# A row-mean kernel rewritten with its own semaphores, behind an empty tile context, with one engine waiting at the end

## The chip, the cores and the metric

The kernel runs on one core of a Trainium2 chip. The metric is the device time of one execution in microseconds (us). Each comparison alternates a kernel with the kernel before on the same chip; medians of the fast runs are quoted. The "span" is the time from the first to the last recorded instruction of an execution; "time outside the span" is the device time less the span.

## The reference

```python
x = np.random.randn(32, 512, 1024).astype(np.float32)      # 67.1 MB
def reference(x):
    return np.mean(np.maximum(x, 0), axis=-1).astype(np.float32)   # 32 x 512
```

16,384 rows of 1024 numbers are clipped at zero and averaged. The output is 64 KB.

## The kernel before

Each of the 128 partitions holds 128 rows. Seven loads of 8.4 MB (16 rows for each partition) go through three buffers; the eighth is cut into pieces of 8, 4, 2 and 1 rows, and the last row into three column pieces. ScalarE takes the even rows, VectorE the odd ones; each does clip and sum in one instruction. GpSimd multiplies the sums by 1/1024, except for the last row, whose final step VectorE does.

```python
    for t in range(full):
        xt = in_pool.tile([P, NB, D], F32, name="xt")
        nc.sync.dma_start(out=xt, in_=xr[:, j0:j0 + NB, :])
        rows(xt, 0, NB, j0)
    # ... row pieces, then column pieces of 512, 256, 256 into `last` ...
    act_row(nc, last[:, :512], last[:, D:D + 1])
    dve_row(nc, last[:, 512:768], last[:, D + 1:D + 2])
    nc.vector.scalar_tensor_tensor(
        out=last[:, 768:], in0=last[:, 768:], scalar=0.0, in1=scale, op0=ALU.max, op1=ALU.mult,
        accum_out=res[:, J - 1:J])       # reads both partial sums, which stand behind the row
    nc.sync.dma_start(out=outr, in_=res)
    pools.close()
    tc.close()          # the close of the tile context ...
    tc.compile()        # ... whose instructions the trace puts at this line, 134
    issue_ahead_of_entry_barrier(nc)     # moves the first load ahead of the entry barrier
```

All semaphores (counters by which one engine waits for another, or for a transfer) are put in by the tile framework. Its close makes SyncE wait for every outstanding semaphore, lets all engines meet, has GpSimd clear the semaphores, and lets all engines meet again.

## Time and profile before

| | before |
|---|---|
| time, median (range) | 163.88 us (163.78 to 164.01) |
| span of the profiled run, its time | 161.80 us, 163.58 us |
| outside the span | 1.78 us |
| DMA engines busy | 96.9% of the span |
| VectorE, ScalarE busy | 74.3 us, 69.2 us |
| second column piece landed, store issued, store landed, span ends | 158.20, 159.36, 160.90, 161.80 us |

The loads fill the span; the ends of it are what a change of semaphores can reach. The prediction shows the lines.

### The profile page before, as it was taken

What the parts mean: (1) busy time and instruction counts of PE and PEld (TensorE: products, weight loads), DVE (VectorE), ACT (ScalarE), POOL (GpSimd) and SP (SyncE); (2) the same over time, 40 slices, a digit from 0 to 9 for tenths busy, and PEclk for the clock granted to TensorE, in tenths of its full rate; (3) what the DMA queues carried; (4) which work ended last, traced back from release to release, by engine and by line L of the source; (5) the groups of instructions that cost most, each with busy time, mean ns of one, the idle gap of its engine ahead of it and who ended that gap; (6) DMA issues with size and microseconds to landing.
All of it is one profiled execution on the core that took longest, in us unless ns stands there. A gap on an engine that the chain in (4) does not pass through costs nothing.

```text
span 161.8 us, 351 instructions
## 1 busy us (share of the span) xinstructions
DVE 74.3 (46%) x132; ACT 69.2 (43%) x131; POOL 1.3 (1%) x8
## 2 busy tenths in 40 slices
DVE  0000049800696008940099202990049800698992
ACT  3000049600694008920099002980049600696882
POOL 1000000000000000000000000000000000000000
DMA  7997997997998998998998998997997996998990
GB/s 259 518 470 308 518 470 308 518 470 324 502 470 356 470 470 356 470 470 356 470 470 360 470 470 356 470 486 340 470 486 340 470 502 300 462 429 381 421 353 20
DMA packets 2162, 67.19 MB, mean 415 GB/s; under 512 B 240, under 2 KB 624, under 8 KB 880
## 3 DMA queue, kind: packets, MB, share of 16 engines
q1 hardware_dynamic: 2160, 67.18, 96.9%
q14 instruction: 2, 0.02, 0.0%
HBM read 67.11 MB, written 0.07 MB: 415 GB/s over the span
## 4 chain that ended last, share of the span: by engine, by line
DMA 84%; DVE 12%; SPq 1%; issue 0%; DVEq 0%
DMA xt<-in_x_dram 56%; DMA last<-in_x_dram 29%; DVE xt L20 11%; SPq L105 1%; SPq L109 0%; DVE last L20 0%; DVE last L126 0%; DVEq L126 0%; DVEq L20 0%; SPq L97 0%; DVEq L134 0%
## 5 line engine op out<-in xcount | busy, mean ns | idle before, releaser
L20 DVE TENSOR_SCALAR_CACHE_REDUCE xt<-xt 128x1024 f32<-128x1024 f32 x64 | 73.4, 1208 | 84.5 <-DMA xt<-in_x_dram 84.2
L15 ACT ACTIVATE xt<-xt 128x1024 f32<-128x1024 f32 x64 | 66.2, 1036 | 88.6 <-DMA xt<-in_x_dram 88.4
L15 ACT ACTIVATION_READ_ACCUMULATOR xt<-xt 128x1 f32 x64 | 12.0, 187 | 0.0
L20 DVE DVE_READ_ACCUMULATOR xt<-xt 128x1 f32 x64 | 5.3, 82 | 0.0
L90 POOL TENSOR_SCALAR res<-sums 128x112 f32<-128x112 f32 (+1 forms) x2 | 0.5, 251 | 155.9 <-DVE xt L20 155.9
L15 ACT ACT_TABLE_LOAD x1 | 1.3, 1283 | 0.8 <-PEq L150 0.8
L15 ACT ACTIVATE last<-last 128x512 f32<-128x512 f32 x1 | 0.6, 629 | 0.0
L20 DVE TENSOR_SCALAR_CACHE_REDUCE last<-last 128x256 f32<-128x256 f32 x1 | 0.4, 420 | 0.2 <-DMA last<-in_x_dram 0.2
L126 DVE SCALAR_TENSOR_TENSOR last<-last,scale 128x258 f32<-128x258 f32 x1 | 0.4, 430 | 0.2 <-DVE last L20 0.2
L81 POOL MEMSET scale<- 128x258 f32 x1 | 0.3, 314 | 0.3 <-POOLq L150 0.3
L121 POOL TENSOR_SCALAR res<-part 128x1 f32<-128x1 f32 x1 | 0.3, 267 | 0.6 <-DVE xt L20 0.6
L15 ACT ACTIVATION_READ_ACCUMULATOR last<-last 128x1 f32 x1 | 0.2, 186 | 0.0
L150 POOL MEMSET const-bfloat16-1.0<- 128x1 bf16 x1 | 0.1, 103 | 0.0
L150 POOL MEMSET const-uint8-127<- 128x1 uint8 x1 | 0.1, 103 | 0.0
L150 POOL MEMSET const-float32-0.0<- 128x1 f32 x1 | 0.1, 99 | 0.2 <-issue 0.2
L150 POOL MEMSET const-float32-1.0<- 128x1 f32 x1 | 0.1, 99 | 0.0
L126 DVE DVE_READ_ACCUMULATOR last<-last,scale 128x1 f32 x1 | 0.1, 86 | 0.0
L20 DVE DVE_READ_ACCUMULATOR last<-last 128x1 f32 x1 | 0.1, 83 | 0.0
## 6 DMA issues: line engine op xcount, KB each, us to landing
xt<-in_x_dram SPq DMA_DIRECT2D x1, 4096.0 KB, 39.0
xt<-in_x_dram SPq DMA_DIRECT2D x1, 2048.0 KB, 43.5
xt<-in_x_dram SPq DMA_DIRECT2D x1, 1024.0 KB, 45.5
xt<-in_x_dram SPq DMA_DIRECT2D x1, 512.0 KB, 46.4
last<-in_x_dram SPq DMA_DIRECT2D x1, 256.0 KB, 46.5
last<-in_x_dram SPq DMA_DIRECT2D x2, 128.0 KB, 42.7
xt<-in_x_dram SPq DMA_DIRECT2D x7, 48.8
out_dram<-res SPq DMA_DIRECT2D x1, 64.0 KB, 1.5
```

The source lines that it names most:

```text
L15: nc.scalar.activation(out=src, in_=src, func=ACT.Relu, accum_out=acc)
L20: nc.vector.tensor_scalar(out=src, in0=src, scalar1=0.0, scalar2=init, op0=ALU.max, op1=ALU.add, accum_out=acc,)
L81: nc.gpsimd.memset(scale, inv)
L90: nc.gpsimd.tensor_scalar(out=res[:, lo:hi], in0=sums[:, lo:hi], scalar1=inv, scalar2=0.0, op0=ALU.mult, op1=ALU.add,)
L105: nc.sync.dma_start(out=xt[:, lo:lo + n, :], in_=xr[:, j0 + lo:j0 + lo + n, :])
L121: nc.gpsimd.tensor_scalar(out=res[:, J - 2:J - 1], in0=part[:, 0:1], scalar1=part[:, 1:2], scalar2=inv, op0=ALU.add, op1=ALU.mult,)
L126: nc.vector.scalar_tensor_tensor(out=last[:, 768:], in0=last[:, 768:], scalar=0.0, in1=scale, op0=ALU.max, op1=ALU.mult, accum_out=res[:, ...
L150: nc = _bacc.Bacc("TRN2", target_bir_lowering=False, num_devices=1)
```

## The change

The intent is to shed the framework's close. The tile context is closed and compiled while it is still empty; after it the same loads and instructions are written with hand-placed semaphores, one for each load, and at the end SyncE alone waits for the store. The core of the diff:

```diff
+    tc.close()
+    tc.compile()
 ...
+    loaded = [nc.alloc_semaphore(f"loaded{i}") for i in range(full + len(row_pieces) + len(col_pieces))]
+    act, dve, pool = (nc.alloc_semaphore(n) for n in ("act", "dve", "pool"))
+    stored = nc.alloc_semaphore("stored")
+    def load(i, dst, src):
+        nc.sync.dma_start(out=dst, in_=src).then_inc(loaded[i], 16)
+    def buf_free(t):
+        if t >= BUFS:
+            nc.sync.wait_ge(act, t - BUFS + 1)
+            nc.sync.wait_ge(dve, t - BUFS + 1)
 ...  (rows and finish wait on `loaded`, `act` and `dve`; all loads are written first)
+    nc.vector.wait_ge(loaded[i + 2], 16)
+    dve_row(nc, last[:, 512:768], last[:, D + 1:D + 2]).then_inc(dve, 1)
+    nc.vector.wait_ge(act, n_done + 1)
+    nc.vector.wait_ge(dve, n_done + 1)
+    nc.vector.wait_ge(loaded[i + 3], 16)
     nc.vector.scalar_tensor_tensor(
 ...
-    nc.sync.dma_start(out=outr, in_=res)
-    pools.close()
-    tc.close()
-    tc.compile()
+    nc.sync.wait_ge(pool, 2)
+    nc.sync.wait_ge(dve, n_done + 2)
+    nc.sync.dma_start(out=outr, in_=res[:, :]).then_inc(stored, 16)
+    used = [s.num for s in (*loaded, act, dve, pool)]
 ...
+    nc.sync.sem_clear(range(used[0], used[-1] + 1))
+    nc.sync.wait_ge(stored, 16).then_inc(stored, -16)
```

More of the change, by code (lines that the diff above doesn't have):

```diff
@@ L13, in act_row @@
 def act_row(nc, src, acc):
-    nc.scalar.activation(out=src, in_=src, func=ACT.Relu, accum_out=acc)
+    return nc.scalar.activation(out=src, in_=src, func=ACT.Relu, accum_out=acc)
 def dve_row(nc, src, acc, init=None):
-    nc.vector.tensor_scalar(
+    return nc.vector.tensor_scalar(
         out=src, in0=src, scalar1=0.0, scalar2=init,
@@ L38, in issue_ahead_of_entry_barrier @@
     assert first.engine == mybir.EngineType.SP and not first.sync_info.on_wait
-    assert all(i.opcode == "DMACopy" or i.engine != first.engine for i in body[:load])
+    assert all(i.opcode in ("Drain", "EventSemaphore") or i.engine != first.engine for i in body[:load])
     del body[load]
@@ L60 @@
     outr = out.flatten().rearrange("(p j) -> p j", p=P, j=J)
-    xlast = xr[:, J - 1, :]
     NB = 16
+    BUFS = 3
     full = J // NB - 1
@@ L69, with sbuf, rows, finish @@
     assert sum(col_pieces) == D
-    pools = ctx.enter_context(ExitStack())
-    in_pool = pools.enter_context(tc.tile_pool(name="in", bufs=3))
-    res_pool = pools.enter_context(tc.tile_pool(name="res", bufs=1))
-    sums = res_pool.tile([P, J], F32)
-    res = res_pool.tile([P, J], F32)
-    part = res_pool.tile([P, 2], F32)
-    last = res_pool.tile([P, D + 2], F32)
-    scale = res_pool.tile([P, D // 4 + 2], F32)
-    nc.gpsimd.memset(scale, inv)
-    def rows(xt, lo, n, j0):
+    def sbuf(name, *shape):
+        return ctx.enter_context(nc.sbuf_tensor(name, list(shape), F32))
+    bufs = [sbuf(f"rows{b}", P, NB, D) for b in range(BUFS)]
+    sums, res, part = sbuf("sums", P, J), sbuf("res", P, J), sbuf("part", P, 2)
+    last = sbuf("last", P, D + 2)
+    scale = sbuf("scale", P, D // 4 + 2)
+    loaded = [nc.alloc_semaphore(f"loaded{i}") for i in range(full + len(row_pieces) + len(col_pieces))]
[7 more added lines that the diff above has]
+            nc.sync.wait_ge(dve, t - BUFS + 1)
+    for t in range(full):
+        buf_free(t)
+        load(t, bufs[t % BUFS][:, :, :], xr[:, t * NB:(t + 1) * NB, :])
+    j0 = full * NB
+    buf_free(full)
+    xt = bufs[full % BUFS]
+    lo, i = 0, full
+    for n in row_pieces:
+        load(i, xt[:, lo:lo + n, :], xr[:, j0 + lo:j0 + lo + n, :])
+        lo, i = lo + n, i + 1
+    c = 0
+    for w in col_pieces:
+        load(i, last[:, c:c + w], xr[:, J - 1, c:c + w])
+        c, i = c + w, i + 1
+    nc.gpsimd.memset(scale[:, :], inv).then_inc(pool, 1)
+    def rows(i, xt, lo, n, j0):
+        nc.scalar.wait_ge(loaded[i], 16)
+        nc.vector.wait_ge(loaded[i], 16)
         for k in range(lo, lo + n):
             j = j0 + k
-            (dve_row if j % 2 else act_row)(nc, xt[:, k, :], sums[:, j:j + 1])
-    def finish(lo, hi):
+            done = (dve_row if j % 2 else act_row)(nc, xt[:, k, :], sums[:, j:j + 1])
+            if k >= lo + n - 2:
+                done.then_inc(dve if j % 2 else act, 1)
+    def finish(after, lo, hi):
+        nc.gpsimd.wait_ge(act, after)
+        nc.gpsimd.wait_ge(dve, after)
         nc.gpsimd.tensor_scalar(
@@ L92, in finish @@
         )
+    nc.vector.wait_ge(pool, 1)
     for t in range(full):
-        j0 = t * NB
-        xt = in_pool.tile([P, NB, D], F32, name="xt")
-        nc.sync.dma_start(out=xt, in_=xr[:, j0:j0 + NB, :])
-        rows(xt, 0, NB, j0)
-    j0 = full * NB
-    xt = in_pool.tile([P, NB, D], F32, name="xt")
-    prev = xt[:, NB - 2, :]
-    lo = 0
-    for n in row_pieces:
-        nc.sync.dma_start(out=xt[:, lo:lo + n, :], in_=xr[:, j0 + lo:j0 + lo + n, :])
-        lo += n
-    c = 0
-    for w in col_pieces:
-        nc.sync.dma_start(out=last[:, c:c + w], in_=xlast[:, c:c + w])
-        c += w
@@ L112 @@
-    finish(0, j0)
-    lo = 0
-    for n in row_pieces[:-1]:
-        rows(xt, lo, n, j0)
-        lo += n
-    finish(j0, j0 + lo)
-    act_row(nc, prev[:, :448], part[:, 0:1])
-    dve_row(nc, prev[:, 448:], part[:, 1:2])
+        rows(t, bufs[t % BUFS], 0, NB, t * NB)
+    finish(full, 0, j0)
+    lo, i = 0, full
+    for n in row_pieces[:-1]:
+        rows(i, xt, lo, n, j0)
+        lo, i = lo + n, i + 1
+    finish(i, j0, j0 + lo)
+    prev = xt[:, NB - 2, :]
+    nc.scalar.wait_ge(loaded[i], 16)
@@ L121 @@
+    act_row(nc, prev[:, :448], part[:, 0:1]).then_inc(act, 1)
+    nc.vector.wait_ge(loaded[i], 16)
+    dve_row(nc, prev[:, 448:], part[:, 1:2]).then_inc(dve, 1)
+    n_done = i + 1
+    nc.gpsimd.wait_ge(act, n_done)
+    nc.gpsimd.wait_ge(dve, n_done)
     nc.gpsimd.tensor_scalar(
         out=res[:, J - 2:J - 1], in0=part[:, 0:1], scalar1=part[:, 1:2], scalar2=inv, op0=ALU.add, op1=ALU.mult,
-    )
-    act_row(nc, last[:, :512], last[:, D:D + 1])
-    dve_row(nc, last[:, 512:768], last[:, D + 1:D + 2])
+    ).then_inc(pool, 1)
@@ L126 @@
+    nc.scalar.wait_ge(loaded[i + 1], 16)
+    act_row(nc, last[:, :512], last[:, D:D + 1]).then_inc(act, 1)
+    nc.vector.wait_ge(loaded[i + 2], 16)
[3 more added lines that the diff above has]
+    nc.vector.wait_ge(loaded[i + 3], 16)
     nc.vector.scalar_tensor_tensor(
-        out=last[:, 768:], in0=last[:, 768:], scalar=0.0, in1=scale, op0=ALU.max, op1=ALU.mult,
+        out=last[:, 768:], in0=last[:, 768:], scalar=0.0, in1=scale[:, :], op0=ALU.max, op1=ALU.mult,
@@ L128 @@
         accum_out=res[:, J - 1:J],
-    )
-    nc.sync.dma_start(out=outr, in_=res)
-    pools.close()
-    tc.close()
-    tc.compile()
+    ).then_inc(dve, 1)
+    nc.sync.wait_ge(pool, 2)
+    nc.sync.wait_ge(dve, n_done + 2)
+    nc.sync.dma_start(out=outr, in_=res[:, :]).then_inc(stored, 16)
+    used = [s.num for s in (*loaded, act, dve, pool)]
+    assert used == list(range(used[0], used[0] + len(used)))
+    nc.sync.sem_clear(range(used[0], used[-1] + 1))
+    nc.sync.wait_ge(stored, 16).then_inc(stored, -16)
```

## The prediction

> **What bounds the kernel now.** I read the views in this order: the page's engine shares and slices, the table of stretches, the chain of waits, then the waits of SyncE's queue and the instructions of the closing line. The page's first parts:
>
> ```profile
> span 161.8 us, 351 instructions
> DVE 74.3 (46%) x132; ACT 69.2 (43%) x131; POOL 1.3 (1%) x8
> ...
> DMA  7997997997998998998998998997997996998990
> ...
> q1 hardware_dynamic: 2160, 67.18, 96.9%
> ```
>
> Neither compute engine is busy half the time; the DMA engines are busy 96.9% of the span, and the row of digits has no hole except at its end. So the stream of loads is the bound, and only what lies before its first byte and after its last one can be changed by a change of waits. Six stretches, cut at places of the chain, put sizes to it (DVE, ACT, POOL busy, clock, DMA share, GB/s):
>
> ```profile
> 0.00:1.00 1.00, 0.00 (x0) 0.22 (x1) 0.43 (x5) 1.00 0.00 0
> 1.00:22.60 21.60, 0.00 (x0) 1.06 (x1) 0.09 (x1) 1.00 1.05 437
> 22.60:158.20 135.60, 73.45 (x128) 67.55 (x129) 0.54 (x3) 1.00 0.99 425
> 158.20:159.40 1.20, 0.87 (x4) 0.40 (x2) 0.23 (x1) 1.00 0.00 0
> 159.40:160.90 1.50, 0.00 (x0) 0.00 (x0) 0.00 (x0) 1.00 0.15 44
> 160.90:161.80 0.90, 0.00 (x0) 0.00 (x0) 0.00 (x0) 1.00 0.00 0
> ```
>
> The reader sees 1.00 us until the first data packet, 157.2 us of saturated loading, 1.20 us of arithmetic on the last row, 1.50 us for the store, and 0.90 us in which nothing at all works. The end of the chain of waits (start, length, what):
>
> ```profile
> 41.91 0.02 issue
> 41.93 9.22 DVE xt L20 x16
> ...
> 100.10 0.03 issue
> 100.12 0.05 DVEq L20
> 100.17 0.07 issue
> 100.24 9.22 DVE xt L20 x16
> ...
> 158.20 0.02 issue
> 158.22 0.44 DVE last L20 x2
> ...
> 158.86 0.43 DVE last L126
> ```
>
> Two prices of a wait stand here. A load that landed at 41.91 was followed by its first VectorE row 0.02 us later: the row carried the wait itself. A load that landed at 100.10 was followed at 100.24, since a semaphore instruction (DVEq L20) stood in front: 0.14 us, so 0.12 us more. And the last 0.9 us, by SyncE's queue and by the closing line:
>
> ```profile
> SPq L134 <- DMA out_dram<-res: 1.0, 1, 1.0
> SPq L134 <- PEq L134: 0.6, 2, 0.4
> ...
> L134 SPq EVENT_SEMAPHORE  x7: 17/27/28, 159.8 to 161.7; - x7
> ...
> L134 POOLq EVENT_SEMAPHORE_RANGE_CLEAR  x1: 95/95/95, 161.4 to 161.4; - x1
> ```
>
> SyncE waits 1.0 us for the store and after it 0.6 us in two meetings of all engines, with a clear of the semaphores between them (161.41).
>
> **What the Trainium skill says.** "DMA: Bandwidth & Descriptors", section Specifications, gives a fabric ceiling of 435 GB/s for 16 engines, and an HBM limit of about 358 GB/s for a core. The trace agrees with the first (437 GB/s in the first stretch; 8.39 MB between landings at 22.60 and 41.91, which is 434 GB/s) and exceeds the second; the measurement decides: there is no bandwidth left to win. "Perfetto Trace Analysis", section Identifying Dependency Chains, says that an instruction with several waits may have EventSemaphore instructions put in front of it; the trace agrees (the DVEq L20 piece, and two more before L126). The same page, section DMA Instruction — HWDGE, says that the profiled length of a DMA instruction ends when the sequencer is free and that the transfer comes after, with a completion that waits for the write. The trace agrees: the store's instruction took 348 ns, its landing came 1.5 us after its start. "Runtime: NRT & Kernel Launch", section The ~15µs preamble/postamble breakdown, lists a closing barrier of about 1.5 us and a reset of semaphores of about 1.5 us outside the kernel. No view of this trace shows these; all it shows is that the profiled run was timed at 163.58 us with a span of 161.80, so 1.78 us lie outside the span.
>
> **The change, part by part.**
>
> 1. *The close after the store goes away (gain on the path).* Now the store lands at 160.90 and the span ends at 161.80: 0.90 us, made of two more SyncE wait instructions for semaphores that were long full, two drains, and two rendezvous around the range clear. Afterwards SyncE alone waits, with one semaphore instruction after the landing, and its own range clear (95 ns at present on GpSimd) is put before that wait, beside the 1.5 us of the store. I charge the one wait 0.02 us to be released and 0.03 us for itself (27 ns median in the closing line's row), 0.05 us. Gain 0.90 - 0.05 = 0.85 us.
>
> 2. *Waits stand alone (loss, partly on the path).* The compile step now runs before these instructions exist, so I take it that nothing folds the written waits into the instructions behind them, and each is a semaphore instruction of its own. By the two prices above that is 0.12 us for each place where a wait that ends last was carried by its instruction. On the path at the end there is exactly one such place: the second piece of the last row, landed at 158.20, VectorE started at 158.22; it would start at 158.34. Before L126 there are two separate semaphore instructions now and the wait for VectorE's own result (158.66 to 158.86) comes last; afterwards three, the first of them (for ScalarE) already met; about the same 0.20 us. Before the store there is a separate wait for VectorE now and there will be one: 0. ScalarE's half row starts 0.1 us later too and ends near 158.70, still before VectorE's piece ends near 158.78: beside the path. Loss 0.12 us.
>
> 3. *The empty context's close at the start (added, hidden).* It is the same drain, rendezvous, clear, rendezvous as in the last 0.65 us of the present span. The first load is still put ahead of the entry barrier, so it starts as now; the second is issued at about 0.78 + 0.65 = 1.4 us, while the first keeps the DMA engines at work until 22.60. Slack 21 us; cost 0. The constant fill on GpSimd (314 ns) and the 1.28 us table load on ScalarE move as well, also in front of a wait that ends at 22.6 us.
>
> 4. *Buffers and semaphores of the loads (moved, hidden).* Each load has its own semaphore, so the last column piece no longer waits 7.2 us for an earlier landing before it is issued; it stands behind 8 MB or more in the same queue in any case. Buffer reuse is the same rule: three buffers, freed by the last ScalarE and VectorE row. A refill is issued at 31.91 when loads for nearly another 30 us are queued (landings at 41.91 and 61.27), so 0.1 us here costs nothing. Cost 0.
>
> 5. *Fewer increments on the rows.* Rows run back to back now (9.22 us for 8 rows) and are off the path. 0.
>
> Sum: -0.85 + 0.12 = -0.73 us, so a span near 161.07 us. With the same time outside the span: 163.9 - 0.73 = 163.17. I lower it by 0.07 for the chance that four engines that are free early shorten what lies outside, and say **163.1 us**.
>
> **Rivals.** *A, the waits are folded after all, or the four early engines hide part of the 1.78 us:* for it speaks that all engines but SyncE would be idle some 1.6 us before the end; against it, that SyncE still ends last and whatever follows must meet it. It would make 162.5 to 163.0. *B, the head is exposed:* if the first load were no longer first, or the DMA engines waited for the second rendezvous, up to 0.65 us would be lost in front of the stream, and the time would be 163.6 to 163.8, so no gain. Against it: the diff keeps the move of the first load, and the first packet started at 1.00 us, 0.2 us after the entry barrier and 1.00 us after the issue, the issue's own latency by all that I see. *C, the table load of ScalarE falls behind the first wait:* then ScalarE's first tile ends 1.3 us later, near 32.5 instead of about 31, and so does the first refill; the queue is full until 61.27, so 0. *D, the stream itself changes:* with other buffer addresses or denser issues the 157.2 us could move; half a percent would be 0.8 us. Against it: the descriptors are the same sizes in the same order on the same queue, and the runs before spread by only 0.23 us.
>
> **Range and chances.** The gain has a ceiling at 0.90 us within the span, and outside it little is plausible; a loss needs B or D. The spread of runs is 0.1 us each way. So 162.5 to 163.6 should hold 8 in 10. A gain over 2% would be 3.3 us, more than the whole 0.90 us of close, the 0.12 to 0.20 us gaps and the 1.78 us outside together; I give it 0.02. Slower by 2% needs a broken stream: 0.01. Within 2%: 0.97.
>
> **What would show it.** Right, if the changed profile has a span of about 161.1 us; the store's landing within 0.1 us of the last instruction's end; no range clear by GpSimd in the last microsecond but one near 1.2 us; the second load issued at 1.3 to 1.8 us; DMA share still 96 to 98%; and VectorE's start on the second column piece 0.12 to 0.15 us after its landing. Step 1 is wrong if anything runs over 0.2 us past the landing; step 2, if that start follows the landing by 0.02 us; step 3, if the first packet starts later than 1.1 us or a slice of the DMA row near 22 us has a hole. The whole is wrong if the time moves without the span, for then the place is outside what I can see.

## More of the kernel before

One more view is needed later: three lines of the timeline, which give start, length, engine, line and operation, and in brackets the idle time before.

```profile
158.57 0.08 DVE L20 DVE_READ_ACCUMULATOR last<-last 128x1 f32 x1
158.86 0.43 DVE L126 SCALAR_TENSOR_TENSOR last<-last,scale 128x258 f32<-128x258 f32 x1 [0.21 <-DVE last L20]
...
159.36 0.35 SPq L130 DMA_DIRECT2D out_dram<-res  x1
```

VectorE's partial sum is ready at 158.65 (158.57 + 0.08), and the final instruction that reads it starts 0.21 us later.

## The result

| | before | changed |
|---|---|---|
| time, median (range) | 163.88 us (163.78 to 164.01) | 162.32 us (162.08 to 162.41) |
| ratio of fast runs, 95% interval | | 0.9902 (0.9885 to 0.9919) |
| span of the profiled run, its time | 161.80, 163.58 us | 161.07, 162.41 us |
| outside the span, mean | 1.78 us (one run; 1.785 in 11 later runs) | 1.31 us (four runs) |

A ratio is the mean time of one kernel's fast runs over that of the other's of the same rounds, so it is not quite the ratio of the medians. The class is "same within 2%", as forecast, but the time of 162.32 lies below the stated range of 162.5 to 163.6: the gain is 1.56 us where 0.78 was forecast (163.88 less 163.1).

The changed kernel's page, first parts (busy time, the DMA share in 40 slices, the queue's share, and the engines' part of the chain of waits):

```profile
span 161.1 us, 336 instructions
DVE 74.3 (46%) x132; ACT 69.2 (43%) x131; POOL 1.3 (1%) x8
...
DMA  7997997997997998999999999999999999899991
...
q1 hardware_dynamic: 2160, 67.18, 97.3%
...
DVE 0%; issue 0%
```

The work and the saturation are as before. The chain of waits is a warning: it stops at VectorE's own result at 158.89 us, just ahead of the final instruction, and goes no further back. It does not mean that loads have left the critical path. The stretches still show it, here the bulk and the end (stretch, length, DVE, ACT, POOL busy, clock, DMA share, GB/s):

```profile
22.30:158.44 136.14, 73.44 (x128) 67.56 (x129) 0.55 (x3) 1.00 0.98 424
158.44:159.50 1.06, 0.86 (x4) 0.39 (x2) 0.21 (x1) 1.00 0.00 0
159.50:161.04 1.54, 0.00 (x0) 0.00 (x0) 0.00 (x0) 1.00 0.15 43
161.04:161.10 0.06, 0.00 (x0) 0.00 (x0) 0.00 (x0) 1.00 0.00 0
```

The 0.90 us in which nothing worked has become 0.03 us (the last stretch was cut at 161.10; the store landed at 161.04 and the span ends at 161.07). The waits of SyncE's queue and the one instruction of the new closing line (duration min/median/max in ns) say the same:

```profile
SPq L172 <- DVE last L165: 46.6, 1, 46.6
SPq L178 <- SPq L178: 1.1, 1, 1.1
SPq L55 <- PEq L55: 0.5, 2, 0.3
...
L178 SPq EVENT_SEMAPHORE  x1: 17/17/17, 161.1 to 161.1; - x1
```

SyncE waits 1.1 us for the store and is done 0.03 us after the landing; its last instruction takes 17 ns of that. The two meetings (L55) now stand at the start, in the first 1.4 us. And the timeline of the tail:

```profile
158.46 0.42 DVE L20 TENSOR_SCALAR_CACHE_REDUCE last<-last 128x256 f32<-128x256 f32 x1 [0.25 <-DMA last<-in_x_dram]
...
158.81 0.08 DVE L20 DVE_READ_ACCUMULATOR last<-last 128x1 f32 x1
158.99 0.43 DVE L165 SCALAR_TENSOR_TENSOR last<-last,scale 128x258 f32<-128x258 f32 x1
...
159.50 0.35 SPq L173 DMA_DIRECT2D out_dram<-res  x1
```

The second column piece landed at 158.44 and VectorE began at 158.46, 0.02 us later as before. The partial sum was ready at 158.89 and the final instruction began 0.10 us later, against 0.21 before. So the span's account, from the landing records and the timeline of the two profiled runs, is:

| piece of the path (us) | before | changed | difference |
|---|---|---|---|
| start to landing of the second column piece | 158.20 | 158.44 | +0.24 |
| landing to partial sum ready | 0.45 | 0.45 | 0 |
| partial sum ready to the final instruction | 0.21 | 0.10 | -0.11 |
| final instruction, and on to the store's issue | 0.50 | 0.51 | +0.01 |
| store issued to landed | 1.54 | 1.54 | 0 |
| store landed to the end of the span | 0.90 | 0.03 | -0.86 |
| outside the span | 1.78 | 1.34 | -0.45 |
| time of the profiled run | 163.58 | 162.41 | -1.17 |

(The differences are those of the unrounded times.) The rows from the landing to the end of the span, the "tail", sum to 3.60 us before and 2.64 us after: -0.96 us. Three rows depart from the forecast: the partial sum to the final instruction (a loss was forecast around there), the time outside the span (0.07 allowed for it) and the shift of the stream (rival D, put at 0).

### The profile page after: what moved, and what is told of

It reads as the page before. It is cut to its first block, busy times and chain, and to the rows that moved or that the text cites. A ratio compares the mean times of both kernels' runs of the same rounds, so it can differ in the third digit from the quotient of the medians.

```text
span 161.1 us, 336 instructions
## 1 busy us (share of the span) xinstructions
DVE 74.3 (46%) x132; ACT 69.2 (43%) x131; POOL 1.3 (1%) x8
## 3 DMA queue, kind: packets, MB, share of 16 engines
q1 hardware_dynamic: 2160, 67.18, 97.3%
## 5 line engine op out<-in xcount | busy, mean ns | idle before, releaser
L20 DVE TENSOR_SCALAR_CACHE_REDUCE rows<-rows 128x1024 f32<-128x1024 f32 x64 | 73.3, 1208 | 84.8 <-DMA rows<-in_x_dram 84.6
L15 ACT ACTIVATE rows<-rows 128x1024 f32<-128x1024 f32 x64 | 66.2, 1036 | 88.2 <-DMA rows<-in_x_dram 88.0
L15 ACT ACTIVATION_READ_ACCUMULATOR rows<-rows 128x1 f32 x64 | 11.9, 187 | 0.0
L20 DVE DVE_READ_ACCUMULATOR rows<-rows 128x1 f32 x64 | 5.3, 83 | 0.0
```

Source lines behind the costliest of these rows:

```text
L15: return nc.scalar.activation(out=src, in_=src, func=ACT.Relu, accum_out=acc)
L20: return nc.vector.tensor_scalar(out=src, in0=src, scalar1=0.0, scalar2=init, op0=ALU.max, op1=ALU.add, accum_out=acc,)
```

## The experiments

Theory A: engines released early do whatever follows their last instruction beside the store, so less remains after the span. Theory B: the time outside the span fell for another reason (chance, the other layout of the program, its start, its semaphores). Twelve runs were made in four calls (sessions, each on one chip). All runs gave correct results, and no result is left out.

**own_again**: the changed kernel, unedited. It was run at another time.

> The changed kernel once more, unedited, for more runs of time and span together. The change took 1.56 us, but the span only about 0.7 to 0.9: the time outside the span (time less span) fell from 1.78 us in the one profiled run of before to 1.28 to 1.35 us in four runs. Theory A (engines that are released early do their closing work beside the store) and theory B (the 0.45 us is a matter of the run or of the program's other parts, such as its blocks, its start or its semaphores) both expect 162.3 us and 1.3 us outside here; a chance of the run would show an outside that scatters between 1.3 and 1.8.

Measured: 162.52 us against 163.65 for the kernel before (11 runs), ratio 0.9929 (0.9918 to 0.9941). Outside the span: 1.29 to 1.33 us in five runs, against 1.74 to 1.82 in the 11 runs of before. The gain outside, 0.47 us, does not scatter. The gain of the span does: here the mean spans are 161.88 and 161.20, 0.68 us apart, so the whole gain was 1.13 us rather than 1.56.

**old_close**: the close of before put back at the end of the changed program.

```diff
-    nc.sync.sem_clear(range(used[0], used[-1] + 1))
     nc.sync.wait_ge(stored, 16).then_inc(stored, -16)
+    nc.all_engine_barrier()
+    nc.gpsimd.sem_clear(range(used[0], used[-1] + 1))
+    nc.all_engine_barrier()
```

> The changed kernel with the close of before put back at its end alone: SyncE waits for the store, then a meeting of all engines, GpSimd's range clear, a second meeting. Both theories expect a span longer by 0.6 to 0.75 us, some 161.7. Theory A: outside the span about 1.75 us again, time 163.4 to 163.6. Theory B: outside stays 1.3 us, time 163.0 to 163.1.

Measured: 163.34 us, ratio to the kernel before 0.9989 (0.9973 to 1.0004). Outside the span 1.78 us on average. The profile's waits of SyncE's queue and the line of the clear:

```profile
SPq L177 <- SPq L177: 1.2, 1, 1.2
...
SPq L180 <- PEq L180: 0.3, 1, 0.3
...
SPq L178 <- PEq L178: 0.2, 1, 0.2
...
L179 POOLq EVENT_SEMAPHORE_RANGE_CLEAR  x1: 135/135/135, 161.1 to 161.1; - x1
```

The two meetings and the clear are back after the store. The landing-to-end piece is 0.72 us (0.90 in the kernel before, where SyncE has one more semaphore wait and one more drain there), and 1.78 us outside came back with it. So the close alone makes nearly the whole difference, in two parts: inside the span and outside it. The empty context, the own semaphores and the new order of issue are worth little by themselves: the tail is 3.31 us here against 3.60 before, with 0.17 of the difference in this last piece and the rest in the waits ahead of the final instruction (treated under late_first). Theory B's layout, start and semaphores are out, for they were all still in this kernel.

**all_held**: no meetings, but each other engine waits for the store last.

```diff
+    for e in (nc.gpsimd, nc.scalar, nc.vector, nc.tensor,):
+        go = nc.alloc_semaphore(f"go_{e.engine.name}")
+        nc.sync.wait_ge(stored, 16).then_inc(go, 1)
+        e.wait_ge(go, 1).then_inc(go, -1)
     nc.sync.wait_ge(stored, 16).then_inc(stored, -16)
```

> The changed kernel, but SyncE hands the store's arrival on to each of the other four engines, which wait for it as their last instruction; no meeting and no clear after it. SyncE needs four more semaphore instructions of about 0.06 us each, so the span should be 0.2 to 0.3 us longer, some 161.3. Theory A: outside about 1.75 us, time 163.0 to 163.1. Theory B: outside 1.3 us, time 162.6.

Measured: 162.87 us (162.73 to 163.04), outside 1.65 us. Merely letting the engines leave late puts most of the 0.47 us back, so theory A holds. It is less than 1.75 since SyncE released the engines one after another: GpSimd left at 160.82, 0.26 us ahead of TensorE.

**pool_held, act_held, dve_held, pe_held**: the same loop with one engine in it.

```diff
+    for e in (nc.gpsimd,):        # or nc.scalar, nc.vector, nc.tensor
```

> The changed kernel; SyncE hands the store's arrival on to GpSimd alone, which waits for it last; ScalarE, VectorE and TensorE still leave early. All four held gave 1.65 us outside the span against 1.31 with none held. Theory A1: one engine's own closing work is the long one; then exactly one of these four single runs shows 1.6 us or more and the other three 1.31 to 1.40, whose sum of excesses is that of all four. Theory A2: every engine but SyncE has a longer close than SyncE; then all four singles show 1.5 to 1.8. In both, the span is 0.05 to 0.1 us longer than the changed kernel's. For GpSimd, which opened and closed the meetings of before, I expect 1.35 under A1.

> As pool_held, with ScalarE alone held until the store. A1: it is one of 1.31 to 1.40 outside the span, or the one of 1.6 and more; A2: 1.5 to 1.8. From all_held, where ScalarE was released at 160.89 and the run ended 1.83 us later, and before, where it was released at 161.77 and the run ended 1.81 us later, the two intervals agree within 0.02 us for ScalarE and differ by 0.04 to 0.14 for the other engines, so my guess for the long one is ScalarE: 1.65 to 1.75 outside the span.

> As pool_held, with VectorE alone held until the store. A1 with ScalarE as the long one: 1.31 to 1.40 us outside the span. A2: 1.5 to 1.8.

> As pool_held, with TensorE alone held until the store (it has no work of its own here and was the last to leave in the kernel before). A1 with ScalarE as the long one: 1.31 to 1.40 us outside the span. A2: 1.5 to 1.8.

Measured, mean outside the span: GpSimd held 1.86 us, TensorE 1.65, ScalarE 1.47, VectorE 1.46; none held 1.31. Times 162.76, 162.79, 162.51 and 162.70. (The times also carry the scatter of the stream; the time outside does not.) My guess of ScalarE was wrong (the 1.83 us in it is 1.85 by the trace: 162.74 less 160.89), and so was A1's picture of a single long engine: each has its own length, SyncE the shortest, as A2 said, though two lie a little under A2's 1.5. In the profile of pool_held the last instructions of GpSimd and SyncE stand side by side:

```profile
L181 POOLq EVENT_SEMAPHORE  x1: 17/17/17, 160.9 to 160.9; - x1
...
L182 SPq EVENT_SEMAPHORE  x1: 17/17/17, 160.9 to 160.9; - x1
```

GpSimd ended at 160.90 and SyncE at 160.94, and yet the run took 162.77, 1.87 us past GpSimd's end; with SyncE last alone (own_again) it took 1.33 us past SyncE's end. From the five runs with one engine at the end I take one constant an engine, the run's time less the end of that engine's last instruction, read from the packed trace (what lies before the first instruction is in all five alike):

| engine | GpSimd | TensorE | ScalarE | VectorE | SyncE |
|---|---|---|---|---|---|
| end of its last instruction to the end of the run, us | 1.87 | 1.67 | 1.49 | 1.46 | 1.33 |

The rule "the run ends at the latest of the five sums" then gives the time of the nine other profiled runs to 0.01 us:

| run | engine that decides, its end + constant | time |
|---|---|---|
| before | GpSimd 161.71 + 1.87 = 163.58 | 163.58 |
| before_again | GpSimd 162.04 + 1.87 = 163.91 | 163.92 |
| old_close | GpSimd 161.48 + 1.87 = 163.35 | 163.35 |
| all_held | TensorE 161.07 + 1.67 = 162.74 | 162.74 |
| changed | SyncE 161.07 + 1.33 = 162.41 (unrounded) | 162.41 |
| late_first | SyncE 161.03 + 1.33 = 162.36 | 162.36 |
| late_first_2 | SyncE 161.25 + 1.33 = 162.59 (unrounded) | 162.59 |
| fill_act | SyncE 160.93 + 1.33 = 162.26 | 162.26 |
| fill_dve | SyncE 161.06 + 1.33 = 162.39 | 162.39 |

The test is sharp for GpSimd, TensorE and SyncE. ScalarE and VectorE decide none of the nine, so their constants rest on one profile each, with the mean time outside of their other runs.

So before the change the run ended on GpSimd, and the change made it end on SyncE, whose constant is 0.54 us smaller. In the profiles of before, GpSimd's last instruction ended 0.09 us ahead of the span's end, which leaves 0.45 us: the drop outside the span. What the engines do in these 1.3 to 1.9 us no record of these traces shows.

**late_first**: the order of the waits ahead of the two last instructions.

```diff
-    nc.vector.wait_ge(act, n_done + 1)
     nc.vector.wait_ge(dve, n_done + 1)
+    nc.vector.wait_ge(act, n_done + 1)
 ...
-    nc.sync.wait_ge(pool, 2)
     nc.sync.wait_ge(dve, n_done + 2)
+    nc.sync.wait_ge(pool, 2)
```

> The changed kernel with the waits before the last VectorE instruction and before the store put in another order, so that the wait that ends last is the one that the instruction itself carries, and the earlier ones stand in the semaphore instruction ahead of it (in the changed profile it is the other way round: VectorE's own result was ready at 158.89, its wait instruction ended at 158.94 and the work began at 158.99; for the store 159.42 and 159.50). If a carried wait is cheaper by the 0.1 us that the load waits showed, each of the two places gives 0.05 to 0.1 us: time lower by 0.1 to 0.2, 162.1 to 162.2. Rival: on the engine's own results the price is in the semaphore's way, not in the extra instruction; then 162.3 as before.

Measured: 162.36 us against 162.52 of own_again on the same chip. The ratios to the kernel before, 0.9918 (0.9905 to 0.9932) and 0.9929 (0.9918 to 0.9941), overlap, so the times alone do not prove it. The timeline does show each place:

```profile
158.88 0.08 DVE L20 DVE_READ_ACCUMULATOR last<-last 128x1 f32 x1
159.00 0.43 DVE L165 SCALAR_TENSOR_TENSOR last<-last,scale 128x258 f32<-128x258 f32 x1
159.35 0.08 DVE L165 DVE_READ_ACCUMULATOR last<-last,scale 128x1 f32 x1
159.46 0.35 SPq L173 DMA_DIRECT2D out_dram<-res  x1
```

The final instruction starts 0.04 us after the partial sum (158.96 to 159.00; 0.10 in the changed kernel), and the store is issued 0.03 us after the result (159.43 to 159.46; 0.08). The wait listed first was carried by the instruction in every such place; the later ones stood in a semaphore instruction ahead of it.

**late_first_2**: the same kernel again.

> late_first once more, for a second profile and more times, since its first result lay only 0.16 us under that of the changed kernel. The tail from the landing of the second column piece to the end of the span should be 2.52 us again (2.63 to 2.64 in four profiles of the changed kernel and of its two fillers), the time outside the span 1.31 to 1.36, and the time below that of the kernel before by 0.96 + 0.11 in the tail and 0.45 outside, 1.5 us, give or take 0.3 for where the stream ends. Rival: the 0.12 us of the tail was scatter; then 2.63.

Measured: tail 2.53 us (2.52 in the first), so the 0.11 us is real inside the tail. The time was 162.48 (161.93 to 162.74), ratio 0.9920 (0.9904 to 0.9936); the stream of the profiled run landed its second column piece at 158.72, the latest of all. The kernel beats the one before clearly, and the changed one by the tail's 0.11 us, which the scatter of the stream hides in the times.

**before_again**: is the stream of the changed kernel really later, as its +0.24 us suggested?

> The kernel before, unedited, for a second profile of it on the chip of the other runs of this call. By the account so far the tail from the landing of the second column piece to the end of the span is 3.60 us (2.63 after the change), time outside the span 1.78. Where the stream ends is open: 158.20 in the first profile of before, 158.14 to 158.53 in those of the changed kernel and its variants. If the stream of the changed kernel is truly later, this profile has its second column piece landed by 158.2 again; if it is scatter from run to run and chip to chip, it lies anywhere between 158.1 and 158.6. Time within 0.3 us of the kernel before, as it is the same.

Measured: 163.77 us; tail 3.60 us again; second column piece landed at 158.53, not 158.20. In the twelve profiles of the changed kernel and its variants it lay between 158.12 and 158.72. So the +0.24 us of the first pair lies within the scatter. The times say the same: in the twelve comparisons of the changed kernel and its variants, the difference of the mean spans less that of the tails leaves -0.32 to +0.28 us for the stream, 0.00 on average (an estimate, since spans are to 0.1 us and each tail is from one profile).

**fill_act, fill_dve**: 24 idle semaphore increments on one engine at the start, to move its instruction fetch.

```diff
+    spare = nc.alloc_semaphore("spare")       # cleared with the others
+    for _ in range(24):
+        nc.scalar.sem_inc(spare, 1)           # fill_dve: nc.vector
```

> The changed kernel with 24 semaphore instructions that do nothing useful (increments of a spare semaphore) on ScalarE before its first wait, hidden behind the first load. In the profiles so far two fetches of 8 KB of instructions, 0.31 us each on a DMA ring, stand in the stream at 65.1 us (86.5 before), and between the landings of the loads around it 19.6 to 19.9 us pass where 19.35 is usual. Theory F: the fetch delays the ring that ends last. If one of the two fetches is ScalarE's, 24 more instructions at two to a row bring it forward by 12 rows, to near 42 us, and some of the excess moves to the load landing near 61. Rival: the fetches belong to other engines, or the excess has another cause; then both stay at 65 and the excess stays with the load landing near 81. Time the same as the changed kernel, 162.3 to 162.6, in either case, since a ring's work is only moved.

> As fill_act, with the 24 spare semaphore instructions on VectorE. Theory F with one fetch for each of the two engines: here the other fetch moves to near 42 us and the first stays. Rival: nothing moves. Time 162.3 to 162.6.

Measured: 162.23 and 162.33 us (before: 163.67 on that chip). The trace's DMA records and landings gave (time between the full landings of neighbouring 8.4 MB loads; 19.35 is usual):

```text
run        fetches at (us)   load 1   load 2   load 3   load 4   load 5
before       86.4   86.6      19.31    19.36    19.35    19.47    19.35
before_again 84.4   87.0      19.32    19.60    19.38    19.92    19.35
changed      65.1   65.2      19.36    19.45    19.86    19.36    19.35
fill_act     28.4   65.0      19.33    19.36    19.94    19.36    19.35
fill_dve     28.7   67.9      19.64    19.36    19.51    19.34    19.36
```

In each run one of the two fetches moved, so one belongs to each engine; they went to 28.5, not to 42 as I had reckoned. The largest excess of each run stands in an interval that holds a fetch, up to 0.6 us in these five runs; the two fetches take 0.31 us each. When VectorE's fetch moved, 0.29 us of excess stood at its new place and 0.16 at the old interval; when ScalarE's did, none was seen at its new place. But in own_again's profile load 1 took 19.57 us, 0.22 over the usual, with no fetch in it, so the one run with VectorE's fetch moved is a hint and no proof. That a fetch causes the excess is not shown; which DMA engine it falls on, why it cost 0.12 us in one profile of before and 0.57 in another, and where the smaller excesses in other intervals come from, is open.

## Why the prediction was wrong

1. *The close (step 1): right.* Forecast -0.85 us, measured -0.86 in the first pair of profiles; old_close showed that 0.69 of it comes from the meetings and the clear (0.72 less 0.03). One reading in the step was off without effect: only one wait instruction for full semaphores followed the landing, at 160.98, since the one before it, at 160.92, was the store's own.
2. *Waits stand alone (step 2): wrong, in sign too.* The step that failed reads "nothing folds the written waits into the instructions behind them". They were folded: VectorE began 0.02 us after the landing, as before. And ahead of the final instruction two of the three waits shared one semaphore instruction, where before two such instructions stood, the first for VectorE's own result: 0.10 us instead of 0.21 (the step had expected about 0.20 there again). So +0.12 was forecast and -0.11 found.
3. *The start (step 3): right.* The second load was issued at 1.43 us (1.4 forecast) and the first packet started at 1.00 us in both. The clear that I expected near 1.2 us was absent, without effect.
4. *Loads and buffers, rows (steps 4 and 5): right.* DMA share 97.3%, refill issued at 31.75 against 31.91, and the last column piece was issued at 112.4 instead of 119.5 without landing earlier.
5. *Outside the span: the mechanism named, the size missed.* "I lower it by 0.07 for the chance that four engines that are free early shorten what lies outside" is the term that was mis-sized; it measured 0.47. Rival A named both misses (waits folded, early engines), as alternatives, and was held down by the argument "SyncE still ends last and whatever follows must meet it". The single-engine runs show why that argument fails: what follows is not the same for each engine, and SyncE's is the shortest. The prediction had named the sign: "The whole is wrong if the time moves without the span"; 0.47 us of it did.

The forecast sum was -0.85 + 0.12 - 0.07 = -0.80 us. The measured sum is -0.96 in the tail and -0.47 outside, -1.43 us, to which the stream's scatter adds: -1.56 in the first comparison, -1.13 in own_again's (where the spans' gain of 0.68 leaves +0.28 for the stream). The range had no room for two errors in the same direction. The span alone had looked like a success: 161.07 forecast, 161.07 measured; but there -0.23 of step 2 and +0.24 of the stream had cancelled. A hit on a sum is no proof of its terms.

On the Trainium skill: the close outside the kernel that "Runtime: NRT & Kernel Launch", section The ~15µs preamble/postamble breakdown, lists (a barrier for all engines, then a reset of semaphores on each) is a candidate for the engines' constants, but no record of these runs shows it, and the page gives no times by engine.

## What to carry to other kernels

At the end of a program, let one engine alone wait for the store, let it be the one with the smallest constant (here SyncE), and let GpSimd leave at least 0.54 us ahead of it (these constants were measured with this program alone); look at the time outside the span as well as the span. Write the wait that will end last as the first in the list, so that the instruction carries it: 0.05 us a place here. When a change is worth less than 1%, compare pieces of the path between fixed events, since the stream of loads alone scattered by 0.6 us between profiles.

## What the Trainium skill lacked or had wrong

- "Runtime: NRT & Kernel Launch" describes the closing stages with one figure for all engines. The runs show that what follows an engine's last instruction differs by engine: 1.87 us for GpSimd, 1.67 TensorE, 1.49 ScalarE, 1.46 VectorE, 1.33 SyncE (each with the same unknown part before the first instruction in it), and that the latest sum sets the time, to 0.01 us in nine other profiled runs. Whether the stages of the page are what follows is not shown.
- "Perfetto Trace Analysis" says that waits may be put in semaphore instructions ahead of an instruction, but not which one stays with it, nor its price: here the first in the program's list stayed, and putting the last-ending wait there gained 0.06 us on VectorE and 0.05 on SyncE.
- "DMA: Bandwidth & Descriptors", section Specifications, gives about 358 GB/s as the HBM limit of one core without its condition; the stream ran at 424 to 440 GB/s in the stretches of these profiles, and at 434 between landings (8.39 MB in 19.35 us). The 435 GB/s of the fabric is the figure that fits. The condition (both cores that share the HBM streaming) stands further down on the same page.
- "Runtime: NRT & Kernel Launch", section Instruction fetch mechanics, calls the cost of a fetch mostly hidden and says nothing of a stream that fills the DMA engines. In the twelve profiles without the filler instructions, two fetches of 8 KB (0.31 us each) stood in an interval between landings that was 0.1 to 0.75 us longer than the usual 19.35; that the fetches made it longer is not shown.
